# A hybrid decoder layer in float32: products moved from GpSimd to VectorE, two steps moved to a later place in the order

## The chip, the cores and the metric

The kernel runs on one core of one Trainium2 chip. The metric is the device time of one execution in microseconds, the median of several runs; lower is better. A profile of one execution, taken by the hardware, stands beside the times.

## What is computed

One decoder layer for 512 tokens of width 2048, float32. The normalised input goes through one wide projection; its columns feed two branches, whose outputs are gated, added, projected and added to the input. The reference, cut to what matters:

```python
xn = rmsnorm(h, norm_w); proj = xn @ w_in
# branch 1: gated linear recurrence, 8 heads of 128
f = lb + (1 - lb) * sigmoid(f_pre); k = 1 - f
#   S_t = diag(f_t) S_{t-1} + k_t i_t^T ;  o_t = S_t^T q_t
o_hg = rmsnorm(o, hg_norm_w) * silu(hg_z);  y_hg = o_hg @ w_branch_hg
# branch 2: sparse attention, 16 heads in 4 groups, rotation on 32 of 128 dims
p_cmp = masked_softmax(q @ kc.T);  o_cmp = p_cmp @ vc   # 31 compressed keys
p = masked_softmax(q @ ks.T);      o_slc = p @ vs       # selected blocks
p = masked_softmax(q @ kw.T);      o_win = p @ vw       # window
o_nsa = (g0 * o_cmp + g1 * o_slc + g2 * o_win) * silu(nsa_z)
y_nsa = o_nsa @ w_branch_nsa
h = h + (g_hg * y_hg + g_nsa * y_nsa) @ w_out;  return rmsnorm(h, final_norm_w)
```

With 512 tokens the selection takes every block that a query may see, so the selected and the window part are both causal attention, with different keys and values.

## The kernel before, in words

Every wide product keeps float32 accuracy by splitting each operand into a high part (a cast on ScalarE) and a low part (a subtraction on VectorE) and running three matmuls (`mm3`, L139 to L141). A chunk of weights, 128x1024 numbers, is loaded by SyncE's queue, cast on ScalarE (L130) and split on VectorE (L131); two chunks are held (`whl`). A chunk feeds eight units of three matmuls.

The stages, in order of time: the start (0 to 62 us) normalises four blocks of 128 tokens (`normalise`), transposes them and multiplies each with the first weight columns; then gates and values by a scheme with seven products for eight (to some 500 us); the recurrence, head by head; the compression of keys and values beside the recurrence's branch product; the attention, group by group (some 1130 to 1660 us); the branch product of the attention, the output product and the last normalisation.

Small work is woven into the projections: `weave` runs a generator of projection units and, after every few units, one step of a side generator. In the recurrence `hg_core(head)`, 17 steps, runs beside the 48 units of `hg_proj(head + 1)`. It builds decays over spans of 2, 4, ... 128 tokens: `grow` (L566 on GpSimd, L567 on VectorE) doubles a span, `decayed` (L576 on GpSimd, L577 on VectorE) makes the scaled operands `qk`, L601 multiplies them on TensorE, L605 puts the result into `ad` by a mask. Two levels share a bank of PSUM. Then come the states (L644 to L648), the output `po`, its square split in two, and, in the last step, the mean over the head by two matmuls with `ones` (L668, L669), the root on ScalarE (L670, with a load of its function table), the reciprocal (L671) and two products on VectorE (L672, L673), and the store.

In the attention `nsa_core(g)`, 48 steps, runs beside the projection of the next group, `nsa_proj(g + 1)`, or beside z and gate units. Per group: scores against the compressed keys and their softmax over `pc`; then per head four score steps (blocks i = 3, 2, 1, 0: scores into a bank of the two `sc` banks, mask and row maximum in one VectorE instruction L921, exponential on ScalarE L925, reciprocal and gate, scaling on GpSimd L930), and six steps that transpose the probabilities (L949), split them and multiply them with the values into `po`. `roped` rotates a projected head: a shuffle, the sine product on GpSimd (L698), cosine product and sum on VectorE. `raw` names rotating tiles of two buffers, used by rotations, z units and the compressed values (`vcz`), which are loaded from `vc_d` by ScalarE's queue.

A scheduler sets each engine's order ahead of time from the program; each engine then runs its instructions strictly in that order, and waits by semaphores.

Of the kernel before, what the change touches and what calls it, by code (L numbers as in the profile page):

```python
# [8 lines left out]
F32 = mybir.dt.float32  # L9
# [6 lines left out]
P = 128  # L16
S = 512
# [58 lines left out]
def body(tc, a, out):  # L76
# [216 lines left out]
    with pool("st_a") as sp:  # L293
# [29 lines left out]
        def normalise(i):  # L323
            x = xt[i]
            ss = sp.tile([P, 2], F32, name="ss", bufs=4)
            h0, h1 = slice(0, D // 2), slice(D // 2, D)
            sq = sp.tile([P, D // 2], F32, name="sq", bufs=1)
            sq2 = sp.tile([P, D // 2], F32, name="sq2", bufs=1)
            nc.scalar.activation(sq, x[:, h1], AF.Square, accum_out=ss[:, 1:2])
            nc.vector.scalar_tensor_tensor(sq2, x[:, h0], 1.0, x[:, h0], op0=OP.mult, op1=OP.mult,  # L330
                                           accum_out=ss[:, 0:1])
            for k0 in (8, 12):
                c = slice(k0 * P, (k0 + 4) * P)
                nc.gpsimd.tensor_tensor(x[:, c], x[:, c], nw[:, c], op=OP.mult)
            nc.vector.tensor_tensor(ss[:, :1], ss[:, :1], ss[:, 1:], op=OP.add)
            nc.scalar.activation(ss[:, :1], ss[:, :1], AF.Sqrt, scale=1.0 / D, bias=epst)
            nc.vector.reciprocal(ss[:, :1], ss[:, :1])
            for k0 in range(0, KD, 4):
                c = slice(k0 * P, (k0 + 4) * P)
                if k0 < 8:  # L340
                    nc.vector.scalar_tensor_tensor(x[:, c], x[:, c], ss[:, :1], nw[:, c], op0=OP.mult, op1=OP.mult)
                else:
                    nc.vector.tensor_scalar(x[:, c], x[:, c], ss[:, :1], None, op0=OP.mult)

# [158 lines left out]
    with pool("hg") as hp:  # L503
        hgw = sv[:, R_HGW:R_HGW + 1]
        heads = {}
        def values(pr):

# [32 lines left out]
        def hg_core(head):  # L540
# [18 lines left out]
            def grow(h):  # L559
# [5 lines left out]
                whole = lambda v: v[:, :, w - 1:w].to_broadcast([P, S // h, w])  # L565
                nc.gpsimd.tensor_tensor(fv[:, :, 0], fv[:, :, 0], whole(pv[:, :, 1]), op=OP.mult)  # L566
                nc.vector.tensor_tensor(pv[:, :, 1], pv[:, :, 1], whole(pv[:, :, 0]), op=OP.mult)  # L567

            def decayed(h):
# [5 lines left out]
                qk = hp.tile([P, S], F32, name="qk", bufs=3)  # L575
                nc.gpsimd.tensor_tensor(half(qk)[:, :, 0], half(kt)[:, :, 0], half(suf)[:, :, 0], op=OP.mult)  # L576
                nc.vector.tensor_tensor(up(tiles(qk)), up(q), up(tiles(pre)), op=OP.mult)  # L577
# [45 lines left out]
            qd = hp.tile([P, 3, P], F32, name="qd", bufs=2)  # L623
            nc.gpsimd.tensor_tensor(kd, kt[:, :3 * P], suf[:, :3 * P], op=OP.mult)
            nc.vector.tensor_tensor(qd, q[:, 1:], tiles(pre)[:, 1:], op=OP.mult)
# [11 lines left out]
            nc.scalar.copy(kn, ps[:, :3 * P])  # L637
            yield
            yield
            ps = lbank()  # L640
# [25 lines left out]
            yield  # L666
            pm = lbank()
            nc.tensor.matmul(pm, lhsT=ones, rhs=sh, start=True, stop=False)  # L668
            nc.tensor.matmul(pm, lhsT=ones, rhs=sl, start=False, stop=True)  # L669
            nc.scalar.activation(ob, pm, AF.Sqrt, bias=epst)  # L670
            nc.vector.reciprocal(ob, ob)  # L671
            nc.vector.scalar_tensor_tensor(ow, ow, hgw, ob, op0=OP.mult, op1=OP.mult)  # L672
            nc.vector.tensor_tensor(ow, ow, zs, op=OP.mult)  # L673
            nc.gpsimd.dma_start(ohg_d[head], ow)

# [17 lines left out]
    def roped(ap, acc, dst):  # L693
# [3 lines left out]
        nc.vector.stream_shuffle(sh, dst[:ROT], mask=list(range(16, 32)) + list(range(16)))  # L697
        nc.gpsimd.tensor_tensor(sh, sh, sin, op=OP.mult)  # L698
        nc.vector.tensor_tensor(dst[:ROT], dst[:ROT], cos, op=OP.mult)
# [119 lines left out]
    def nsa_proj(g):  # L819
        raw = ap.tile([P, 4, 2, DH], F32, name="vraw")  # L820
        for b in range(2):
            nc.scalar.dma_start(raw[:, :, b], v_d[1 + b, :, :, g * DH:(g + 1) * DH].rearrange("i p c -> p i c"))
        vh = ap.tile([P, 4, 2, DH], F32R, name="vh", bufs=2)
        vl = ap.tile([P, 4, 2, DH], F32R, name="vl", bufs=2)
        f = lambda t: t.rearrange("p j e c -> p (j e c)")
        split(f(vh), f(vl), f(raw))
        q = []
# [21 lines left out]
    def nsa_core(g):  # L849
# [47 lines left out]
        p3l = ap.tile([P, 2, HPG, P], F32R, name="p3l")  # L897
        o3 = ap.tile([P, HPG, P], F32, name="o3")
        for h in range(HPG):
            qh, ql = q[h]  # L900
            sc = {}
            for i in (3, 2, 1, 0):
# [29 lines left out]
            if h == 0:  # L932
                cmp_t()
                yield
            po = psum("po")
            mm3(po, vcz[0][:, h], vcz[1][:, h], ph, pl, True, False)
            pend = None

            def pv_mm(parts, hi, lo, last):
                for n, (j, b) in enumerate(parts):  # L940
                    w = slice(n * (4 - j) * P, (n + 1) * (4 - j) * P)
                    mm3(po[:, j * P:], vh[:, j, b], vl[:, j, b], hi[:, w], lo[:, w], False, last)

            for parts in (((3, 0), (3, 1)), ((2, 0), (2, 1)), ((1, 0),), ((0, 0),), ((1, 1),), ((0, 1),)):
                ps = tbank()
# [8 lines left out]
                else:  # L954
                    hi = ap.tile([P, o], F32R, name=f"pth{o}", bufs=o // 256)
                    lo = ap.tile([P, o], F32R, name=f"ptl{o}", bufs=o // 256)
                    split(hi, lo, ps[:, :o])
                    if pend:
                        pv_mm(*pend, False)
                    pend = (parts, hi, lo)  # L960
                yield
            pv_mm(*pend, True)
            ow = ap.tile([P, 384], F32, name="ow", bufs=2)
            nc.vector.tensor_copy(ow, po[:, :384])
            nc.scalar.copy(o3[:, h], po[:, 384:])
            nc.gpsimd.dma_start(ons_d[g * HPG + h][:, :384], ow)
            yield

        ps = sbank()
# [9 lines left out]
    for g in range(GROUPS - 1):  # L979
        weave(nsa_proj(g + 1), 128, nsa_core(g), 48)  # L980
    
# [3 lines left out]

    weave(last(), 112, nsa_core(GROUPS - 1), 48)
    nsa.close()
# [118 lines left out]
```

## Time and profile before

| | |
|---|---|
| median of 3 runs | 2109.39 us (2108.59 to 2112.3) |
| the profiled execution | 2108.82 us |
| its span, first to last instruction | 2106.7 us |
| TensorE busy | 2062.0 us, 98% |
| VectorE busy | 1209.0 us, 57%, 1875 instructions |
| ScalarE busy | 816.5 us, 39% |
| GpSimd busy | 322.4 us, 15%, 411 instructions |
| granted clock of TensorE | 0.996 of full |

A matmul is listed from its start to its modelled end, and the next one starts before that end; so the engine reads as busy until the last one in flight is through, and a wait shorter than that doesn't show. A float32 matmul that isn't split shows as two passes. The trace names for each idle time the instruction that ended it.

### The profile page before, as it was taken

The numbers are of one execution on the slowest core, as the hardware profiler recorded it, in microseconds if no ns is written. First come the engines' busy times: TensorE is split into PE (matmuls) and PEld (weight loads), VectorE is DVE, ScalarE is ACT, GpSimd is POOL, SyncE is SP. The second block draws the span as 40 slices with busy tenths as digits, with TensorE's granted clock in tenths as the row PEclk, the third lists the DMA queues.
The fourth block names the chain that finished last, engine by engine and source line by source line (L and its number), as shares of the span: only waits on it lengthen the run. The fifth ranks groups of instructions, "written<-read, shape, count | busy, mean of one in ns | idle before, by whom it ended". The sixth has DMA issues, their size and how long they took to land.

```text
span 2106.7 us, 26671 instructions
## 1 busy us (share of the span) xinstructions
PE 2062.0 (98%) x10304; PEld 1721.2 (82%) x10304; DVE 1209.0 (57%) x1875; ACT 816.5 (39%) x1267; POOL 322.4 (15%) x411
## 2 busy tenths in 40 slices
PE   7999999999999999999999999999999999999998
PEld 6888888888888778878888887877878888888887
DVE  7687778745456655566545665657654453433333
ACT  4454444532233233344323444445445432222232
POOL 2000000003233432100002222213212100000000
PEclk9999999999999999999999999999999999999999
DMA  6325243332323222566752222222223394445232
GB/s 184 100 105 180 100 152 114 121 101 74 96 83 93 76 76 85 167 188 202 247 164 85 74 73 85 68 84 64 78 75 92 90 304 132 149 140 212 98 130 90
DMA packets 306595, 254.46 MB, mean 121 GB/s; under 512 B 10666, under 2 KB 263411, under 8 KB 305827
## 3 DMA queue, kind: packets, MB, share of 16 engines
q1 hardware_dynamic: 282980, 202.55, 31.8%
q0 software_dynamic: 8096, 26.28, 3.4%
q10 hardware_dynamic: 15392, 23.92, 3.3%
q8 instruction: 81, 1.33, 0.3%
q14 instruction: 46, 0.38, 0.1%
HBM read 222.25 MB, written 30.47 MB: 120 GB/s over the span
## 4 chain that ended last, share of the span: by engine, by line
PE 82%; DVE 7%; issue 4%; ACT 3%; DMA 3%; POOL 1%; SPq 0%; ACTq 0%; DVEq 0%; POOLq 0%
PE pj L139 17%; PE pj L141 17%; PE pj L140 17%; PE sc L214 4%; PE pt L214 4%; PE sc L215 2%; PE pt L215 2%; PE sc L141 2%; PE sc L139 2%; PE sc L140 2%; PE po L140 1%; DVE whl L131 1%; PE po L139 1%; PE po L141 1%; PE pt L949 1%
## 5 line engine op out<-in xcount | busy, mean ns | idle before, releaser
L139 PE MATMUL pj<-xhl,whl 128*128 128x512 f32 x1344 | 538.5, 401 | 0.0
L141 PE MATMUL pj<-xhl,whl 128*128 128x512 f32 x1344 | 527.7, 393 | 0.8 <-DVE whl L131 0.8
L140 PE MATMUL pj<-xhl,whl 128*128 128x512 f32 x1344 | 525.2, 391 | 0.0
L131 DVE TENSOR_TENSOR whl<-wr,whl 128x1024 fp32r<-128x1024 f32 x244 | 303.8, 1245 | 373.2 <-ACT whl L130 372.5
L130 ACT CAST whl<-wr 128x1024 fp32r<-128x1024 f32 x244 | 256.5, 1052 | 563.3 <-PE pj L141 446.8
L141 PEld LDWEIGHTS pj<-xhl,whl 128*128 128x128 f32 x1344 | 252.3, 188 | 56.6 <-DVE whl L131 2.0
L140 PEld LDWEIGHTS pj<-xhl,whl 128*128 128x128 f32 x1344 | 252.9, 188 | 46.4
L139 PEld LDWEIGHTS pj<-xhl,whl 128*128 128x128 f32 x1344 | 252.7, 188 | 46.1
L135 ACT CAST whl<-xt 128x1024 fp32r<-128x1024 f32 x75 | 78.6, 1052 | 97.7 <-PE pt L215 33.1
L136 DVE TENSOR_TENSOR whl<-xt,whl 128x1024 fp32r<-128x1024 f32 x75 | 91.5, 1223 | 39.3 <-ACT whl L135 39.2
L930 POOL TENSOR_SCALAR s<-s,sm 128x512 f32<-128x512 f32 (+3 forms) x128 | 82.2, 655 | 149.4 <-DVE sm L928 89.9
L139 PE MATMUL pj<-onh,whl 128*128 128x512 f32 x256 | 99.6, 389 | 0.0
L140 PE MATMUL pj<-onl,whl 128*128 128x512 f32 x256 | 99.6, 389 | 0.0
L141 PE MATMUL pj<-onh,whl 128*128 128x512 f32 x256 | 99.6, 389 | 0.0
L136 DVE TENSOR_TENSOR ptl<-pt,pth 128x512 fp32r<-128x512 f32 (+1 forms) x80 | 50.5, 633 | 69.3 <-ACT pth L135 68.6
L925 ACT ACTIVATE s<-s,mx 128x512 f32<-128x512 f32 (+3 forms) x128 | 70.9, 555 | 43.8 <-DVE mx L923 39.0
L135 ACT CAST pth<-pt 128x512 fp32r<-128x512 f32 (+1 forms) x80 | 43.5, 544 | 96.1 <-PE pt L949 95.7
L201 DVE TENSOR_TENSOR xt<-xt 128x1024 f32<-128x1024 f32 x64 | 77.5, 1219 | 0.6
L921 DVE CUSTOM_DVE_ANT_0 s<-sc,cf 128x512 f32<-128x512 f32 (+3 forms) x128 | 59.3, 483 | 20.1 <-PE sc L141 19.4
L698 POOL TENSOR_TENSOR rsh<-rsh,rope 32x512 f32<-32x512 f32 x28 | 42.2, 1507 | 183.8 <-DVE rsh L697 166.3
L566 POOL TENSOR_TENSOR suf<-suf,pre 128x256 f32<-128x256 f32 x56 | 51.8, 926 | 116.7 <-DVE pre L549 94.6
L131 DVE TENSOR_TENSOR cl<-wr,ch 128x1024 fp32r<-128x1024 f32 x32 | 39.1, 1223 | 44.6 <-ACT ch L130 44.6
(431 smaller groups left out, 4004.9 us busy)
## 6 DMA issues: line engine op xcount, KB each, us to landing
wr<-in_w_in_dram SPq DMA_DIRECT2D x172, 512.0 KB
xt<-in_w_in_dram SPq DMA_DIRECT2D x32, 1024.0 KB
wr<-in_w_branch_nsa_dram SPq DMA_DIRECT2D x32, 512.0 KB
wr<-in_w_out_dram SPq DMA_DIRECT2D x32, 512.0 KB
wr<-in_cmp_k_w_dram SPq DMA_DIRECT2D x16, 512.0 KB
wr<-in_w_branch_hg_dram SPq DMA_DIRECT2D x16, 512.0 KB
wr<-in_cmp_v_w_dram SPq DMA_DIRECT2D x16, 512.0 KB
gat_d<-wr POOLq DMA_DIRECT2D x20, 256.0 KB, 3.0
```

The costliest lines, as they stand in the source:

```text
L130: nc.scalar.copy(hi[:, :n], raw[:, :n])
L131: nc.vector.tensor_tensor(lo[:, :n], raw[:, :n], hi[:, :n].bitcast(F32), op=OP.subtract)
L135: nc.scalar.copy(hi, src)
L136: nc.vector.tensor_tensor(lo, src, hi.bitcast(F32), op=OP.subtract)
L139: nc.tensor.matmul(acc, lhsT=lh, rhs=rh, start=start, stop=False, **kw)
L140: nc.tensor.matmul(acc, lhsT=lh, rhs=rl, start=False, stop=False, **kw)
L141: nc.tensor.matmul(acc, lhsT=ll, rhs=rh, start=False, stop=stop, **kw)
L201: nc.vector.tensor_tensor(dst, dst, more, op=OP.add)
L214: nc.tensor.matmul(av, lhsT=l0, rhs=r, start=start, stop=False, skip_group_check=True)
L215: nc.tensor.matmul(av[:, 0], lhsT=l1, rhs=r[:, 0], start=False, stop=stop, skip_group_check=True)
L925: nc.scalar.activation(s[:, b], s[:, b], AF.Exp, scale=SCALE, bias=mx[:, b:b + 1], accum_out=sm[:, b:b + 1])
L930: nc.gpsimd.tensor_scalar(s[:, b], s[:, b], sm[:, b:b + 1], 1.0, op0=OP.mult, op1=OP.mult)
```

## The change

- Start: all four products with the norm weight are on VectorE; before, two were on GpSimd and VectorE scaled their results.
- Recurrence: the GpSimd products of `grow`, `decayed` and `kd` are on VectorE. The normalisation of a head (two mean matmuls to the store) becomes a function that runs in the next head's step 13, between its `kd` transposes and its states; the last head's runs at its own end.
- Attention: sine product and scaling are on VectorE. The first bank of block i = 2 comes from the projection's three banks. The products of probabilities with values are put in a queue `due` and run one or two steps later; a head's last two run in the next head's score steps. The values of a group are loaded as two halves into `raw` tiles. A core has 46 steps.

```diff
-            for k0 in (8, 12):
-                nc.gpsimd.tensor_tensor(x[:, c], x[:, c], nw[:, c], op=OP.mult)
...
-                if k0 < 8:
-                    nc.vector.scalar_tensor_tensor(x[:, c], x[:, c], ss[:, :1], nw[:, c], op0=OP.mult, op1=OP.mult)
-                else:
-                    nc.vector.tensor_scalar(x[:, c], x[:, c], ss[:, :1], None, op0=OP.mult)
+                nc.vector.scalar_tensor_tensor(x[:, c], x[:, c], ss[:, :1], nw[:, c], op0=OP.mult, op1=OP.mult)
...
-                nc.gpsimd.tensor_tensor(fv[:, :, 0], fv[:, :, 0], whole(pv[:, :, 1]), op=OP.mult)
+                nc.vector.tensor_tensor(fv[:, :, 0], fv[:, :, 0], whole(pv[:, :, 1]), op=OP.mult)
...
-                nc.gpsimd.tensor_tensor(half(qk)[:, :, 0], half(kt)[:, :, 0], half(suf)[:, :, 0], op=OP.mult)
+                nc.vector.tensor_tensor(half(qk)[:, :, 0], half(kt)[:, :, 0], half(suf)[:, :, 0], op=OP.mult)
...
-            nc.gpsimd.tensor_tensor(kd, kt[:, :3 * P], suf[:, :3 * P], op=OP.mult)
+            nc.vector.tensor_tensor(kd, kt[:, :3 * P], suf[:, :3 * P], op=OP.mult)
...
             yield
+            if left:
+                left.pop()()
             yield
...
-            pm = lbank()
...
-            nc.gpsimd.dma_start(ohg_d[head], ow)
+            def normed():
+                pm = lbank()
...
+                nc.gpsimd.dma_start(ohg_d[head], ow)
+            left.append(normed)
+            if head == HG - 1:
+                left.pop()()
...
-        nc.gpsimd.tensor_tensor(sh, sh, sin, op=OP.mult)
+        nc.vector.tensor_tensor(sh, sh, sin, op=OP.mult)
...
-        raw = ap.tile([P, 4, 2, DH], F32, name="vraw")
-        for b in range(2):
-            nc.scalar.dma_start(raw[:, :, b], v_d[1 + b, :, :, g * DH:(g + 1) * DH].rearrange("i p c -> p i c"))
...
+        for b in range(2):
+            raw = ap.tile([P, S], F32, name="raw", bufs=2)
+            rv = raw.rearrange("p (i c) -> p i c", i=4)
+            nc.scalar.dma_start(rv, v_d[1 + b, :, :, g * DH:(g + 1) * DH].rearrange("i p c -> p i c"))
+            split(vh[:, :, b], vl[:, :, b], rv)
...
+        def pv_next():
+            if not due:
+                return
+            h, po, parts, hi, lo, last = due.pop(0)
+            for n, (j, b) in enumerate(parts):
+                w = slice(n * (4 - j) * P, (n + 1) * (4 - j) * P)
+                mm3(po[:, j * P:], vh[:, j, b], vl[:, j, b], hi[:, w], lo[:, w], False, last)
+            if last:
...
+                if i > 1:
+                    pv_next()
...
-                        ps = sbank()
+                        ps = bank() if i == 2 and b == 0 else sbank()
...
-                    nc.gpsimd.tensor_scalar(s[:, b], s[:, b], sm[:, b:b + 1], 1.0, op0=OP.mult, op1=OP.mult)
+                    nc.vector.tensor_scalar(s[:, b], s[:, b], sm[:, b:b + 1], None, op0=OP.mult)
...
+                    if m == 2:
+                        po = psum("po")
+                        mm3(po, vcz[0][:, h], vcz[1][:, h], ph, pl, True, False)
+                    elif m > 2:
+                        pv_next()
+                    due.append([h, None, parts, hi, lo, m == 5])
...
-        weave(nsa_proj(g + 1), 128, nsa_core(g), 48)
+        weave(nsa_proj(g + 1), 128, nsa_core(g), 46)
```

**The order of instructions.** Line numbers of the changed kernel are its own: `kt` to `qk` stand there at L542 to L572, the masked copies at L583 to L600, the normalisation at L667 to L672, the states at L641 to L645.

VectorE, the first operations of a head of the recurrence, before:

```order
L549 TENSOR_SCALAR pre<-sg,omlb,lbt 128x512
L552 TENSOR_TENSOR qf<-qf,pre 128x4x64
L671 RECIPROCAL ob<-ob 128x512
L567 TENSOR_TENSOR pre<-pre 128x256
L131 TENSOR_TENSOR whl<-wr,whl 128x1024
L672 SCALAR_TENSOR_TENSOR ow<-ow,sv,ob 128x512
L577 TENSOR_TENSOR qk<-qf,pre 128x128x2
L673 TENSOR_TENSOR ow<-ow,zs 128x512
L588 COPY_PREDICATED ad<-cm,sc 128x256
L567 TENSOR_TENSOR pre<-pre 128x128x2
L590 COPY_PREDICATED ad<-cm,sc 128x128
```

and now:

```order
L544 TENSOR_SCALAR pre<-sg,omlb,lbt 128x512
L547 TENSOR_TENSOR qf<-qf,pre 128x4x64
L561 TENSOR_TENSOR suf<-suf,pre 128x256
L562 TENSOR_TENSOR pre<-pre 128x256
L571 TENSOR_TENSOR qk<-kt,suf 128x128x2
L572 TENSOR_TENSOR qk<-qf,pre 128x128x2
L561 TENSOR_TENSOR suf<-suf,pre 128x128x2
L562 TENSOR_TENSOR pre<-pre 128x128x2
L571 TENSOR_TENSOR qk<-kt,suf 128x64x4
L572 TENSOR_TENSOR qk<-qf,pre 128x64x4
L131 TENSOR_TENSOR whl<-wr,whl 128x1024
L583 COPY_PREDICATED ad<-cm,pt 128x256
```

The reciprocal and the two products of the head before have left the place between the first links; the GpSimd products (`suf`, and `qk` from `kt`) stand in it.

VectorE, between the levels and the end of a head, before:

```order
L605 COPY_PREDICATED ad<-cm,pt 128x16x16
L131 TENSOR_TENSOR whl<-wr,whl 128x1024 x2
L537 TENSOR_TENSOR zs<-pj,zs 128x512
L648 SCALAR_TENSOR_TENSOR st<-st,pre,sc 128x128 x2
L131 TENSOR_TENSOR whl<-wr,whl 128x1024
L136 TENSOR_TENSOR sl<-ob,sh 128x512
```

and now:

```order
L619 TENSOR_TENSOR kd<-kt,suf 128x384
L600 COPY_PREDICATED ad<-cm,sc 128x16x16
L620 TENSOR_TENSOR qd<-qf,pre 128x384
L131 TENSOR_TENSOR whl<-wr,whl 128x1024 x2
L670 RECIPROCAL ob<-ob 128x512
L131 TENSOR_TENSOR whl<-wr,whl 128x1024
L671 SCALAR_TENSOR_TENSOR ow<-ow,sv,ob 128x512
L645 SCALAR_TENSOR_TENSOR st<-st,pre,sc 128x128
L672 TENSOR_TENSOR ow<-ow,zs 128x512
L645 SCALAR_TENSOR_TENSOR st<-st,pre,sc 128x128
L532 TENSOR_TENSOR zs<-pj,zs 128x512
L136 TENSOR_TENSOR sl<-ob,sh 128x512
```

The normalisation of the head before (L670 to L672) now stands ahead of and between the two state additions (L645).

VectorE at the start of the second group of the attention, before:

```order
L131 TENSOR_TENSOR whl<-wr,whl 128x1024
L179 TENSOR_TENSOR raw<-pj,raw 128x512
L876 TENSOR_TENSOR pc<-pt,cf 128x512
L136 TENSOR_TENSOR vczl<-raw,vczh 128x512
L877 TENSOR_REDUCE cst<-pc 128x16
L878 TENSOR_TENSOR pc<-pc,cst 128x512
L921 ISA s_9846,mx<-sc,cf 128x512
L921 ISA mx 128x1
L921 ISA s_9846,mx<-sc,cf 128x512
L921 ISA mx 128x1
```

and now, in two pieces with one weight split between them:

```order
L179 TENSOR_TENSOR raw<-pj,raw 128x512
L136 TENSOR_TENSOR vl<-raw,vh 128x4x128
L879 TENSOR_TENSOR pc<-pt,cf 128x512
L880 TENSOR_REDUCE cst<-pc 128x16
L881 TENSOR_TENSOR pc<-pc,cst 128x512
L942 ISA s_9847,mx<-sc,cf 128x512
L942 ISA mx 128x1
L136 TENSOR_TENSOR vl<-raw,vh 128x4x128
L942 ISA s_9847,mx<-sc,cf 128x512
L942 ISA mx 128x1
L944 TENSOR_SCALAR mx<-mx 128x2
L883 TENSOR_TENSOR pc<-pc,cf 128x512
```

```order
L884 TENSOR_REDUCE cst<-pc 128x16
L131 TENSOR_TENSOR whl<-wr,whl 128x1024
L136 TENSOR_TENSOR vczl<-raw,vczh 128x512
L885 TENSOR_SCALAR cst<-cst 128x16
L948 RECIPROCAL sm<-sm 128x2
L942 ISA s_9881,mx<-pj,cf 128x384
```

The split of the compressed values (`vczl`) has moved behind the row maxima of the first scores; the two splits of the group's values (`vl`) now wait for loads into `raw`. On ScalarE the cast of the second half of the values stands ahead of the exponential over `pc`, and the cast of the compressed values ahead of the first exponentials of the scores.

## Rows read from the trace of the kernel before

**Rows 1.** Stretches: length, busy PE, PEld, DVE, ACT, POOL (instructions), clock, DMA share, GB/s.
```profile
0.00:62.00 62.00, 49.81 (x284) 44.47 (x285) 49.25 (x66) 27.64 (x48) 14.60 (x14) 0.92 0.52 156
...
500.00:895.00 395.00, 387.25 (x2124) 323.20 (x2123) 226.91 (x312) 129.24 (x176) 114.82 (x124) 1.00 0.32 95
...
1130.00:1660.00 530.00, 518.10 (x2520) 428.28 (x2519) 316.96 (x775) 247.20 (x511) 128.72 (x182) 1.00 0.27 78
...
1850.00:1900.00 50.00, 50.00 (x222) 41.38 (x222) 18.61 (x22) 11.99 (x13) 0.00 (x0) 1.00 0.49 150
```

**Rows 2.** Waits of TensorE: who ended them, us in total, times, longest.
```profile
PE sc L139 <- DVE mx L921: 8.9, 6, 2.5
PE sc L601 <- DVE ad L605: 7.4, 7, 1.3
PE pt L349 <- DVE xt L341: 3.6, 1, 3.6
PE pt L349 <- issue: 3.4, 2, 1.8
PE pt L349 <- DVE xt L343: 1.7, 1, 1.7
PE sc L139 <- ACT fh L135: 1.7, 1, 1.7
PE po L140 <- DVE ptl L136: 1.6, 3, 0.5
PE po L139 <- ACT pch L135: 1.2, 2, 1.0
```

**Rows 3.** VectorE in order of time, a head of the recurrence: start, duration, instruction.
```profile
642.26 0.42 DVE L567 TENSOR_TENSOR pre<-pre 128x256 f32<-128x256 f32 x1 [0.56 <-POOL suf L566]
642.61 0.72 DVE L605 COPY_PREDICATED ad<-cm,sc 128x256 f32<-128x256 uint8 x1
```

**Rows 4.** TensorE in order of time, the level matmuls just behind that.
```profile
643.47 1.08 PE L601 MATMUL sc<-qk 128*128 128x64 f32 x8 [1.33 <-DVE ad L605]
```

**Rows 5.** ScalarE and VectorE in order of time, the start of an attention group.
```profile
1282.62 0.62 ACT L135 CAST vczh<-raw 128x512 fp32r<-128x512 f32 x1 [5.03 <-DMA raw<-vc_d]
...
1283.32 0.69 DVE L136 TENSOR_TENSOR vczl<-raw,vczh 128x512 fp32r<-128x512 f32 x1 [3.74 <-ACT vczh L135]
```

**Rows 6.** VectorE by line and shape: busy us, mean ns of one, idle before.
```profile
L131 DVE TENSOR_TENSOR whl<-wr,whl 128x1024 fp32r<-128x1024 f32 x244 | 303.8, 1245 | 373.2 <-ACT whl L130 372.5
...
L699 DVE TENSOR_TENSOR raw<-raw,rope 32x512 f32<-32x512 f32 x24 | 31.0, 1291 | 0.2
...
L671 DVE RECIPROCAL ob<-ob 128x512 f32<-128x512 f32 x8 | 26.8, 3346 | 0.7 <-ACT ob L670 0.7
...
L672 DVE SCALAR_TENSOR_TENSOR ow<-ow,sv,ob 128x512 f32<-128x512 f32 x8 | 9.5, 1192 | 0.0
...
L343 DVE TENSOR_SCALAR xt<-xt,ss 128x512 f32<-128x512 f32 x8 | 7.5, 974 | 1.9 <-POOL xt L334 1.9
...
L341 DVE SCALAR_TENSOR_TENSOR xt<-xt,ss,nw 128x512 f32<-128x512 f32 x8 | 5.9, 768 | 2.7 <-POOL nw L305 2.7
...
L547 DVE TENSOR_SCALAR kt<-sg,nomlb,omlb 128x512 f32<-128x512 f32 x8 | 4.3, 542 | 0.0
...
L335 DVE TENSOR_TENSOR ss<-ss 128x1 f32<-128x1 f32 x4 | 3.7, 925 | 1.7 <-ACT sq L329 1.5
...
L699 DVE TENSOR_TENSOR craw<-craw,rope 32x512 f32<-32x512 f32 x4 | 2.7, 678 | 1.1 <-DMA rope<-in_cf_dram 1.0
```

**Rows 7.** ScalarE in order of time, the end of a head of the recurrence.
```profile
671.29 1.05 ACT L130 CAST whl<-wr 128x1024 fp32r<-128x1024 f32 x1 [0.98 <-PE pj L141]
...
672.86 1.28 ACT L670 ACT_TABLE_LOAD   x1
674.15 0.69 ACT L670 ACTIVATE ob<-pt,epst 128x512 f32<-128x512 f32 x1
```

**Rows 8.** Issues of transfers in the attention: KB each, median us to landing.
```profile
z_d<-raw POOLq DMA_DIRECT2D x8, 256.0 KB, 3.2
```

More of the change, by code (lines that the diff above doesn't have):

```diff
@@ L331, in normalise @@
                                            accum_out=ss[:, 0:1])
-            for k0 in (8, 12):
-                c = slice(k0 * P, (k0 + 4) * P)
-                nc.gpsimd.tensor_tensor(x[:, c], x[:, c], nw[:, c], op=OP.mult)
             nc.vector.tensor_tensor(ss[:, :1], ss[:, :1], ss[:, 1:], op=OP.add)
@@ L505, in body @@
         heads = {}
+        left = []
         def values(pr):
@@ L666, in hg_core @@
             yield
-            pm = lbank()
[L668 to L673, printed above, removed]
-            nc.gpsimd.dma_start(ohg_d[head], ow)
+            def normed():
+                pm = lbank()
+                nc.tensor.matmul(pm, lhsT=ones, rhs=sh, start=True, stop=False)
+                nc.tensor.matmul(pm, lhsT=ones, rhs=sl, start=False, stop=True)
+                nc.scalar.activation(ob, pm, AF.Sqrt, bias=epst)
+                nc.vector.reciprocal(ob, ob)
+                nc.vector.scalar_tensor_tensor(ow, ow, hgw, ob, op0=OP.mult, op1=OP.mult)
+                nc.vector.tensor_tensor(ow, ow, zs, op=OP.mult)
+                nc.gpsimd.dma_start(ohg_d[head], ow)
+            left.append(normed)
+            if head == HG - 1:
+                left.pop()()
         weave(hg_proj(0), 0)
@@ L819, in nsa_proj @@
     def nsa_proj(g):
-        raw = ap.tile([P, 4, 2, DH], F32, name="vraw")
-        for b in range(2):
-            nc.scalar.dma_start(raw[:, :, b], v_d[1 + b, :, :, g * DH:(g + 1) * DH].rearrange("i p c -> p i c"))
         vh = ap.tile([P, 4, 2, DH], F32R, name="vh", bufs=2)
         vl = ap.tile([P, 4, 2, DH], F32R, name="vl", bufs=2)
-        f = lambda t: t.rearrange("p j e c -> p (j e c)")
-        split(f(vh), f(vl), f(raw))
+        for b in range(2):
[3 more added lines that the diff above has]
+            split(vh[:, :, b], vl[:, :, b], rv)
         q = []
@@ L898, in nsa_core @@
         o3 = ap.tile([P, HPG, P], F32, name="o3")
+        due = []
+        def pv_next():
[6 more added lines that the diff above has]
+            if last:
+                ow = ap.tile([P, 384], F32, name="ow", bufs=2)
+                nc.vector.tensor_copy(ow, po[:, :384])
+                nc.scalar.copy(o3[:, h], po[:, 384:])
+                nc.gpsimd.dma_start(ons_d[g * HPG + h][:, :384], ow)
         for h in range(HPG):
@@ L929, in nsa_core @@
                 for b in range(2):
-                    nc.gpsimd.tensor_scalar(s[:, b], s[:, b], sm[:, b:b + 1], 1.0, op0=OP.mult, op1=OP.mult)
+                    nc.vector.tensor_scalar(s[:, b], s[:, b], sm[:, b:b + 1], None, op0=OP.mult)
+                if h == 0 and i == 1:
+                    cmp_t()
                 yield
[L932 to L944, printed above, removed]
+            for m, parts in enumerate((((3, 0), (3, 1)), ((2, 0), (2, 1)), ((1, 0),), ((0, 0),), ((1, 1),), ((0, 1),))):
                 ps = tbank()
@@ L954, in nsa_core @@
                 else:
-                    hi = ap.tile([P, o], F32R, name=f"pth{o}", bufs=o // 256)
-                    lo = ap.tile([P, o], F32R, name=f"ptl{o}", bufs=o // 256)
+                    hi = ap.tile([P, o], F32R, name=f"pth{o}", bufs=2)
+                    lo = ap.tile([P, o], F32R, name=f"ptl{o}", bufs=2)
                     split(hi, lo, ps[:, :o])
-                    if pend:
-                        pv_mm(*pend, False)
-                    pend = (parts, hi, lo)
-                yield
[L962 to L966, printed above, removed]
+                    if m == 2:
[4 more added lines that the diff above has]
+                    due.append([h, None, parts, hi, lo, m == 5])
+                    if m >= 2:
+                        for d in due:
+                            d[1] = po
+                yield
+        while due:
             yield
+            pv_next()
+        yield
         ps = sbank()
@@ L984, in last @@
         yield from merge_gates(NG, NG + 6, ap, "raw")
-    weave(last(), 112, nsa_core(GROUPS - 1), 48)
+    weave(last(), 112, nsa_core(GROUPS - 1), 46)
     nsa.close()
```

## The prediction, made before the changed kernel was run

> **What bounds the kernel now.** I read the busy time by stage first. Late in the program, in the last branch product, nothing disturbs TensorE: 222 matmuls of 512 columns in 50 us, 0.225 us each, the clock at full speed [rows 1]. The same engine is busy for nearly all of every other stage, so the reader should look at what is missing: 12.2 us of 62 at the start, 7.8 of 395 in the recurrence, 11.9 of 530 in the attention [rows 1]. VectorE is busy for 57% of the recurrence and 60% of the attention. So the end is set by TensorE, and the only time to be had are its waits; work taken off GpSimd is worth nothing by itself.
>
> The second view is who TensorE waited for [rows 2]. Recurrence: 7.4 us, 7 times, L601 on VectorE's L605. Attention: 8.9 us in six waits of scores for a score bank (L139 on L921), 1.6 for low halves of probabilities, 1.2 for the compressed branch. Start: 3.6 until the norm weight is broadcast, then 3.4 and 1.7. Compression: 1.7, once. Third, I followed one wait of each kind. In the recurrence VectorE stood 0.56 us for GpSimd's `suf` product, then did `pre`, and only then emptied the bank of the level before [rows 3]; TensorE, 1.33 us idle, wanted that bank [rows 4]. So GpSimd is on the path there, through VectorE's queue. At the start of a group VectorE stood 3.74 us for the split of the compressed values, because ScalarE had stood 5.03 us for their load [rows 5].
>
> **The change part by part.** The profiled execution took 2108.8 us (span 2106.7 and 2.1 around it); the median of the runs is 0.6 above it.
>
> Start. VectorE now does four products with the weight per block of tokens, where it did two and two scalings after GpSimd. The eight scalings took 0.97 us each and four one-column sums 0.93 each while GpSimd ran [rows 6]; eight more products at about 0.77, as the two that stay, and sums that no longer wait at some 0.2 (an estimate: one column is next to nothing) make 7.8+3.7 into 6.2+0.8, 4.5 us less work on VectorE. Against it: in the first block the first low half of the weights now stands behind two more products, 1.5 us. The 3.6 us stay. Of the 5.1 us behind them at most all goes; at worst 2 us are added. I take 4, near the gain, since VectorE has hardly a pause in this stage (49 of 62 us, [rows 1]) and loses more work than it is held back.
>
> Recurrence, what goes. The three GpSimd products per level stand in VectorE's queue, so nothing there waits for GpSimd; in the order, the chain of the levels runs without the reciprocal between its first links. A level is then five operations of some 0.45 us, as the products and copies of [rows 3] are where nothing disturbs them (0.42), and a share of the weight split (1.25, [rows 6]), under 3 us, while TensorE has nine wide matmuls (2.0 us) and 0.9 us of its own per level. I count the 7.4 us as gone. Heads need some 6 us more of VectorE, 14 products at 0.45, in 44 us: 57% becomes about 70%, hidden.
>
> Recurrence, what comes. The normalisation of a head (reciprocal 3.35, product 1.19 [rows 6]) now runs between the state products of the next. VectorE's order there is reciprocal, weight split, product, first state addition; TensorE's third state product waits for that addition. Count from the end of the two mean matmuls. TensorE has 28 wide matmuls (6.3 us) and six small ones of two passes, 0.135 us a pass by [rows 4], 1.6: it comes to the wait after 7.9 us. The split waits for ScalarE's cast, which waits until the weight chunk in use is spent: 18 wide matmuls and two small, 4.6 us, the cast 1.05 as in [rows 7], then split 1.2, product 1.2, addition 0.35: 8.4 to 8.5 us. Through the root instead: table load 1.28 and root 0.69 [rows 7], reciprocal 3.35, split, product, addition: 8.1 plus latencies. So TensorE waits about 0.6; with the second addition behind one more product I take 0.7, times 8 heads 5.6. Bounds: 0 if the split comes early, 1.9 a head if VectorE comes to the reciprocal 2 us late. Net: -2, between -7.4 and +8.
>
> Rotation. The sine product moves to VectorE (28 x about 0.68), while its cosine product no longer runs beside GpSimd: 1.29 us then, 0.68 where it didn't [rows 6]. 19 us come, 15 go: nothing. In the compression stage the chain to the first frame gets shorter by the GpSimd hop: -0.5 of the 1.7.
>
> Attention. The scaling of probabilities costs VectorE 0.54 for 512 columns (a scaling of that shape, [rows 6]), by width 43 us for all 128, off GpSimd; with the rotation 60% becomes about 67%, hidden by TensorE's 530 us unless it bunches. The first score bank of the second block is now taken from the projection's three banks, and products of probabilities come one or two steps later, the last two in the next head. That removes the reason for 1.6 and most of 8.9. Not all: at a group's start the values are now loaded into the two rotating `raw` tiles, behind the store of the z unit, which takes 3.2 us to land [rows 8], and the compressed values wait for one of these tiles; in the new order VectorE and ScalarE each have a wait for such loads in their queue. The 3.74 us pause is then moved behind the first scores, but followed by the compressed probabilities that TensorE must transpose. Of the 11.7 us shown I let 8.5 go. Bounds: -11.7, and +3 if every group start is as late as the worst.
>
> Sum: -4 -2 -0.5 -8.5 = -15, from 2108.8 to 2093.8; as a median 2094.
>
> **Rivals.** (A) No new wait appears: all of 5.1, 7.4, 1.7 and 11.7 goes, 25.9 us: 2082.9, as a median 2083.5. For it: each is a queue that the change shortens. Against: the new queues above.
> (B) The reciprocal is the new wait, 1.9 us a head, 15 us in place of 7.4: +7.6, with the rest -5.4, 2104. It decides where VectorE comes more than about 1 us late to the reciprocal; two weight splits stand before it.
> (C) Slower: VectorE becomes the bound in the four score steps of a head. They hold the row maxima, scalings (2.7 us), a rotation chain (five operations of 0.7, 3.4) and one or two weight splits (1.25 each); with row maxima of about the scalings' size, 2.7 to 4, and small operations some 14 us, while TensorE needs some 12 (33 wide matmuls of the projection, 7.4, and about 4.5 of scores and values). If that excess of 2.3 us per head is not made up in the six transposing steps, where VectorE has less, but met at a bank, it costs 16 x 2.3 = 37 us in place of 11.7: +25, with the rest -6.5, 2127. It decides once VectorE is later than two steps, 5 us, behind.
> (D) Stores issued by GpSimd are held back by VectorE's new scalings, and the raw tiles come free late. A scaling pair is 1.1 us and a score step's set 2.7; at three group starts the latter is 8 us, nearly all that I took from the attention: 2102. The Trainium skill has the mechanism: SBUF — State Buffer, Who interferes with whom, says that tensor_scalar can enter a two-port mode that shuts GpSimd out of the shared ports, and with it the descriptors of its stores. No row here shows a store held back: issue to landing is 3.2 us in the median [rows 8]. By that page's 620 to 3100 ns my estimate would be 2.5 us a store, 7 us at three group starts.
>
> **How the numbers follow.** Chances: forecast 0.55, A 0.17, B 0.15, C 0.07, D 0.06. 0.2% is 4.2 us, about what a measurement here can tell: faster means below 2105. Forecast, A and D are faster, B half of the time: 0.84. Same is the middle of B, 0.07. Slower is C and B's end, 0.09. The range 2080 to 2107 holds the forecast, B, D and nearly all of A; it leaves out C and the ends of A and B.
>
> **What the new profile would show.** Right: no wait of the level matmuls (before: L601) for VectorE; no product of probabilities waiting for a low half; the 12.2 us idle of the start near 8. New waits of about 0.7 us at the third state product, and waits on transposes of compressed probabilities at group starts. Wrong: waits for weight splits in the attention (C), state products waiting for over 1.5 us (B), or group starts without any wait (A).

## The result, and the profile after

| | before | after |
|---|---|---|
| median | 2108.99 us (2107.38 to 2112.3) | 2085.39 us (2082.56 to 2087.05, 4 runs) |
| ratio to before, 95% interval | | 0.9885 [0.9867, 0.9903] |
| span of the profiled execution | 2106.7 us | 2085.2 us |
| VectorE busy | 1209.0 us | 1247.2 us |
| GpSimd busy | 322.4 us | 78.9 us |

The change makes the kernel 1.15% faster. The time lies inside the range of the prediction (2080 to 2107), 8.6 us below its likeliest value of 2094 and 1.9 above rival A's 2083.5. The profiled execution of the changed kernel is the longest of its four (2087.05 us), so the two spans differ by 21.5 us where the medians differ by 23.6.

Busy time by stretch in the changed kernel (columns as in [rows 1]; the stages come a few us earlier now):

```profile
0.00:62.00 62.00, 54.35 (x310) 48.92 (x311) 46.71 (x74) 27.41 (x49) 3.34 (x6) 0.92 0.52 156
500.00:895.00 395.00, 391.07 (x2135) 328.37 (x2134) 249.80 (x429) 132.89 (x183) 11.76 (x22) 1.00 0.35 99
1130.00:1660.00 530.00, 525.45 (x2579) 438.35 (x2578) 345.17 (x928) 250.19 (x522) 20.86 (x37) 1.00 0.29 82
1850.00:1900.00 50.00, 50.00 (x222) 41.39 (x222) 18.85 (x22) 11.98 (x13) 0.00 (x0) 1.00 0.45 139
```

TensorE misses 7.7 us of the start instead of 12.2, 3.9 of the second stretch instead of 7.8, 4.6 of the third instead of 11.9. Of the 3.9 us, 3.7 are the wait for the compression's first frame, which now falls into this stretch. VectorE rises to 63% and 65% of the second and third: more work, and hidden. Who TensorE waited for, in the changed kernel (compare [rows 2]):

```profile
PE sc L139 <- ACT fh L135: 3.7, 1, 3.7
PE pt L343 <- DVE xt L337: 3.1, 1, 3.1
PE pj L139 <- ACT wfh L130: 2.4, 1, 2.4
PE pt L895 <- DVE pc L888: 1.7, 2, 1.0
PE sc L139 <- DVE mx L942: 1.4, 1, 1.4
PE pj L141 <- DVE whl L131: 1.3, 3, 0.5
PE sc L215 <- DVE eh L136: 1.3, 2, 0.8
PE pt L895 <- DVE sm L948: 1.3, 1, 1.3
```

The 7.4 us of the level matmuls are gone (L601 before, L596 now: no line). The 8.9 us for score banks are 1.4. Transposes of the compressed probabilities (L895) are new, 3.0 us. One wait has grown: the first compression matmul waits 3.7 us for the cast of the frame (`fh`), where it waited 1.7. At the start the transposes behind the first wait hardly any more, and a wait of 2.4 us for the cast of the first weights (`wfh`) is new.

To place gains in stages I cut each trace at the same events of TensorE. S: start to the first matmul of the recurrence. R: seven head periods. L: first matmul of the last head to the first compression matmul. C: from there to the first score matmul of the first group (against the compressed keys). A: to the attention's branch product. The rest is 358.0 us in every run. The kernel before was timed again beside each batch of kernels and read 2109.5 to 2112.2 us there, so the ratio compares better than the median.

| kernel | S | R | L | C | A | median | ratio to before |
|---|---|---|---|---|---|---|---|
| before | 481.5 | 328.8 | 89.1 | 240.5 | 608.9 | 2108.99 | |
| after | 477.6 | 320.1 | 92.0 | 239.9 | 597.5 | 2085.39 | 0.9885 [0.9867, 0.9903] |
| products_only | 475.5 | 320.8 | 90.8 | 239.7 | 606.1 | 2092.44 | 0.9911 [0.9896, 0.9926] |
| order_only | 481.9 | 320.8 | 89.7 | 242.6 | 599.3 | 2092.36 | 0.9909 [0.9895, 0.9924] |
| u_rec_pool | 476.3 | 320.7 | 91.7 | 240.4 | 596.7 | 2084.69 | 0.9873 [0.9859, 0.9888] |
| u_norm_end | 475.0 | 320.8 | 90.4 | 239.4 | 597.9 | 2082.9 | 0.9867 [0.9851, 0.9883] |
| u_start_pool | 479.6 | 320.1 | 92.1 | 241.0 | 597.0 | 2088.99 | 0.9901 [0.9886, 0.9916] |
| u_scale_pool | 475.1 | 320.1 | 92.2 | 239.8 | 600.4 | 2086.86 | 0.9892 [0.9878, 0.9907] |
| u_bank | 473.3 | 320.1 | 91.5 | 239.5 | 598.5 | 2084.5 | 0.9884 [0.9867, 0.99] |
| u_pv | 474.0 | 320.1 | 91.8 | 240.2 | 598.6 | 2084.12 | 0.9883 [0.9868, 0.9898] |
| fill10 | 477.3 | 320.2 | 90.7 | 236.4 | 597.9 | 2081.84 | 0.9869 [0.9856, 0.9883] |
| own_tile | 476.7 | 320.2 | 91.4 | 238.3 | 605.2 | 2091.54 | 0.9917 [0.9903, 0.993] |
| both | 478.6 | 320.2 | 90.9 | 237.4 | 604.2 | 2086.81 | 0.9896 [0.9882, 0.9909] |
| early_load | 475.2 | 320.1 | 90.9 | 235.5 | 592.6 | 2075.06 | 0.9831 [0.9818, 0.9845] |

Reading scale: A of the five kernels with the attention code of the changed one (after, u_rec_pool, u_norm_end, u_start_pool, fill10) lies between 596.7 and 597.9. S scatters far more (below), so parts are judged by their own stage, not by the median. The 21.5 us between the two spans are S -3.8, R -8.7, L +3.0, C -0.5, A -11.4. The cuts shift some work: in the new order the two mean matmuls of the seventh head run behind R, in the eighth head (0.5 us from R to L), and in the changed kernel eight projection matmuls that stood in C stand in L (1.8 us).

### The profile page after: what moved, and what is told of

Its sections match the earlier page's. It is cut to its first block, busy times and chain, and to the rows that moved or that the text cites. A ratio compares the mean times of both kernels' runs of the same rounds, so it can differ in the third digit from the quotient of the medians.

```text
span 2085.2 us, 26314 instructions
## 1 busy us (share of the span) xinstructions
PE 2057.3 (99%) x10304; PEld 1723.8 (83%) x10304; DVE 1247.2 (60%) x2147; ACT 813.8 (39%) x1271; POOL 78.9 (4%) x135
## 4 chain that ended last, share of the span: by engine, by line
PE 37%; issue 16%; DMA 2%; DVE 1%; ACT 1%; POOL 1%; ACTq 0%; SPq 0%; DVEq 0%; POOLq 0%
PE pj L141 9%; PE pj L140 9%; PE pj L139 9%; PE sc L139 2%; PE sc L140 2%; PE sc L141 2%; PE po L139 1%; PE po L141 1%; PE po L140 1%; DMA zr<-z_d 1%; PE pt L139 1%; PE pt L140 1%; PE pt L141 1%; PE pt L960 1%; DMA wr<-in_cmp_v_w_dram 0%
## 5 line engine op out<-in xcount | busy, mean ns | idle before, releaser
L131 DVE TENSOR_TENSOR whl<-wr,whl 128x1024 fp32r<-128x1024 f32 x244 | 298.2, 1222 | 394.1 <-ACT whl L130 393.9
L136 DVE TENSOR_TENSOR whl<-xt,whl 128x1024 fp32r<-128x1024 f32 x75 | 91.5, 1223 | 39.9 <-ACT whl L135 39.8
L131 DVE TENSOR_TENSOR cl<-wr,ch 128x1024 fp32r<-128x1024 f32 x32 | 39.2, 1225 | 49.6 <-ACT ch L130 49.4
L942 DVE CUSTOM_DVE_ANT_0 s<-sc,cf 128x512 f32<-128x512 f32 (+3 forms) x112 | 51.1, 475 | 27.9 <-PE sc L141 27.9
L130 ACT CAST ch<-wr 128x1024 fp32r<-128x1024 f32 x32 | 33.6, 1049 | 61.5 <-PE sc L141 43.3
L139 PEld LDWEIGHTS pj<-onh,whl 128*128 128x128 f32 x256 | 48.0, 188 | 10.1
L141 PEld LDWEIGHTS pj<-onh,whl 128*128 128x128 f32 x256 | 48.0, 188 | 10.0
```

What stands on the lines that cost most here:

```text
L130: nc.scalar.copy(hi[:, :n], raw[:, :n])
L131: nc.vector.tensor_tensor(lo[:, :n], raw[:, :n], hi[:, :n].bitcast(F32), op=OP.subtract)
L136: nc.vector.tensor_tensor(lo, src, hi.bitcast(F32), op=OP.subtract)
L139: nc.tensor.matmul(acc, lhsT=lh, rhs=rh, start=start, stop=False, **kw)
L141: nc.tensor.matmul(acc, lhsT=ll, rhs=rh, start=False, stop=stop, **kw)
L942: nc.vector.tensor_tensor_reduce(out=s[:, b], in0=pb[b], in1=mk, scale=1.0, scalar=NEG, op0=OP.add, op1=OP.max, accum_out=mx[:, b:b + 1])
```

## The experiments

**The two halves.** One kernel has only the products on VectorE, in the old order; the other has the new order, with all products left on GpSimd.

products_only, on the kernel before:
```diff
# shortened: the operations alone, not the lines
-  nc.gpsimd.tensor_tensor(...) / nc.gpsimd.tensor_scalar(s[:, b], ...)   # start, recurrence, rotation, scaling
+  nc.vector.tensor_tensor(...) / nc.vector.tensor_scalar(s[:, b], ...)
```


> The kernel before with the products alone moved to VectorE (start, recurrence, sine, scaling); normalisation, products of probabilities, score banks and value tiles as before. Theory Q (GpSimd's products hold TensorE up through VectorE's queue): the start gains 3 to 4 us, the 7.4 us of waits of the level matmuls go to under 2, the attention gains 1 to 3 because its waits for score banks stay: 2094 to 2100. Rival O (where the long normalisation and the products of probabilities stand in the order is what counts, whichever engine does the products): the start's 3 to 4 us alone, the level matmuls still wait over 5 us behind the reciprocal: 2103 to 2107.

order_only, on the kernel after: the same lines from `nc.vector` back to `nc.gpsimd`.

> The changed kernel with all moved products back on GpSimd (start, recurrence, sine, scaling); only the order, the third score bank and the value tiles are changed. Theory Q: no gain at the start, the level matmuls keep 4 us or more of their 7.4 us of waits, the attention gains 5 to 9: 2096 to 2102. Rival O: recurrence and attention gain nearly all that they gained in the change, 8.7 and 11.4 us: 2088 to 2092.

Measured: each half gives 0.9% alone, together 1.15%. In R each half has the whole gain (320.8 both; 320.1 together), so neither theory holds there: each part alone is enough. The attention is divided: the products bring 2.9 us, the order 9.7. TensorE's waits in the attention of products_only, then of order_only:

```profile
PE sc L139 <- DVE mx L915: 9.1, 5, 2.5
```
```profile
PE pt L901 <- DVE mx L950: 2.9, 4, 1.2
PE sc L139 <- DVE mx L948: 2.1, 1, 2.1
```

The waits for score banks need the new order; moving products leaves them as they were.

**Undoing one part in the recurrence.** u_rec_pool puts `grow`, `decayed` and `kd` back on GpSimd; u_norm_end lets each head normalise at its own end.

```diff
-                nc.vector.tensor_tensor(fv[:, :, 0], fv[:, :, 0], whole(pv[:, :, 1]), op=OP.mult)
+                nc.gpsimd.tensor_tensor(fv[:, :, 0], fv[:, :, 0], whole(pv[:, :, 1]), op=OP.mult)
... # the same for the product into qk and for kd
```


> The changed kernel with the recurrence's products alone back on GpSimd. Theory Q: VectorE waits for GpSimd before it empties the level's bank, TensorE waits again 4 to 8 us: 2090 to 2093. Rival O: the chain has room without the reciprocal, no wait comes back: 2085 to 2087.

```diff
-            if left:
-                left.pop()()
...
-            left.append(normed)
-            if head == HG - 1:
-                left.pop()()
+            normed()
```


> The changed kernel with the normalisation of a head back at the end of its own head, the products staying on VectorE. Theory Q: the 5 us of the normalisation stand in the chain of the levels, but that chain has about 5 us to spare: 0 to 2 us slower than the changed kernel, 2085 to 2088. Rival O: the level matmuls wait again, 6 to 9 us: 2091 to 2095.

Measured: R 320.7 and 320.8 against 320.1, and no level matmul waits in either. Two things stood in VectorE's queue ahead of the bank that TensorE wanted, the wait for GpSimd [rows 3] and the reciprocal of 3.35 us between the first links; taking away either is enough. The wait that I had expected at the third state product exists in no kernel with the new order, so the move of the normalisation costs nothing there; with the products on VectorE it brings at most 0.7 us of R, of which 0.5 are the two mean matmuls that fall behind R.

**Undoing one part at the start and in the attention.**

u_start_pool, the start's products back to the old form:
```diff
+            for k0 in (8, 12):
+                nc.gpsimd.tensor_tensor(x[:, c], x[:, c], nw[:, c], op=OP.mult)
... # and VectorE scales these two, as before
```


> The changed kernel with the start's second half of products with the norm weight back on GpSimd. If the start's gain comes from these products: the first projection ends some 3 us later, 2088 to 2090. If it comes from elsewhere (another order of loads): 2084 to 2087.

u_scale_pool, the scaling of probabilities back on GpSimd:
```diff
-                    nc.vector.tensor_scalar(s[:, b], s[:, b], sm[:, b:b + 1], None, op0=OP.mult)
+                    nc.gpsimd.tensor_scalar(s[:, b], s[:, b], sm[:, b:b + 1], 1.0, op0=OP.mult, op1=OP.mult)
```


> The changed kernel with the scaling of probabilities back on GpSimd. Theory Q: transposes come steps after the scaling, so nothing waits for GpSimd; VectorE gets 43 us of 530 back but its two-input operations wait beside GpSimd: within 2 us of the changed kernel, 2084 to 2088. Rival (the scaling's latency on GpSimd held up transposes): 3 to 8 us slower, 2088 to 2094.

u_bank, both score banks of block i = 2 from the two:
```diff
-                        ps = bank() if i == 2 and b == 0 else sbank()
+                        ps = sbank()
```


> The changed kernel with both score banks of the second block from the two sc banks, as before. If the third bank removes the waits for score banks: 4 to 8 us come back as waits of score matmuls for row maxima, 2089 to 2094. If the later place of the products of probabilities removes them: 2085 to 2087.

u_pv, products of probabilities at their old place, 48 steps a core:
```diff
-                if i > 1:
-                    pv_next()
...
+                    if pend:
+                        pv_mm(*pend, False)
+                    pend = (parts, hi, lo)
... # the transposes of the compressed probabilities go back to a step of their own, too
```


> The changed kernel with the products of probabilities at their old place, one step behind their transposes and all within their head; third bank and scaling on VectorE stay. If the delay is what removes TensorE's waits for low halves: 2 to 5 us slower, 2087 to 2091, with waits of po matmuls for ptl. If it removes the waits for score banks too: 6 us slower or more.

Measured: with the old start the first projection ends at 60.8 us in u_start_pool, 60.4 in order_only and 61.4 in the kernel before; with the new one at 56.6 to 58.8 in all eleven kernels. The start is worth some 3 to 4 us. Scaling on GpSimd costs 2.8 us of A. The transposes of the compressed probabilities then wait 3.5 us, for other instructions than the 3.0 us above, and scores wait 2.5 us for banks in place of 1.4; 1.0 of the 2.8 us is busy time and shows in no wait:

```profile
PE pt L895 <- DVE mx L944: 3.5, 4, 1.9
```

The third bank and the delayed products are worth 1.0 and 1.1 us, hardly outside the scatter of A. Without the third bank some waits for score banks come back (u_bank), but the 3.0 us of the transposes go:

```profile
PE sc L139 <- DVE mx L942: 3.9, 3, 2.6
```

Without the delay no product of probabilities waits for a low half (`ptl`), so the sign that I had named for it is missing. As in the recurrence, each edit could hide the other; own_tile, below, has both and is only 0.9 us of A faster than products_only, which has neither. So these two edits, which I thought would bring the attention's gain, are not what brought most of it.

**What is left, and the value tiles.** fill10 runs ten units of the branch product between the first frame and the first compression matmul. own_tile gives the values tiles of their own again, out of `raw` (for space `vraw` and `ow` have one buffer). The kernel called both has the two edits.

```diff
+        filled(10)
```


> The changed kernel with ten units of the value projection put ahead of the first compression matmuls. There TensorE now waits 3.7 us for the first frame, whose cast stands on ScalarE behind a weight cast that waits 5.3 us for its load. If the wait is the frame's lateness: it goes, 2 to 4 us faster, 2081 to 2084. If it is the stage's loads (two weight streams through three tiles): the wait moves to a weight cast and the time stays, 2084 to 2087.

```diff
-            raw = ap.tile([P, S], F32, name="raw", bufs=2)
+            raw = ap.tile([P, S], F32, name="vraw", bufs=1)
...
-                ow = ap.tile([P, 384], F32, name="ow", bufs=2)
+                ow = ap.tile([P, 384], F32, name="ow", bufs=1)
```


> The changed kernel with a tile of its own for the values of a group, in place of the rotating raw tiles (one buffer of the store tile ow is given up for the room). If the loads into raw tiles cause the remaining waits at group starts (the transposes of the compressed probabilities, 3.0 us): they go, 2 to 3 us faster, 2082 to 2084. If the compressed values' own load causes them: 2084 to 2087.

> Both of these. If each removes its wait: 5 to 7 us faster than the changed kernel, 2078 to 2081; if neither: 2084 to 2087.

Measured for fill10: no wait for `fh`; C falls by 3.5 us and L by 1.3, as the first expectation said. The grown wait comes from the order on ScalarE. In the changed kernel the frame's casts stand behind a weight cast that waits for its load (ScalarE in order of time):

```profile
888.34 1.04 ACT L130 CAST whl<-wr 128x1024 fp32r<-128x1024 f32 x1 [5.26 <-DMA wr<-in_w_in_dram]
889.29 1.30 ACT L135 CAST fh<-fr 128x248 fp32r<-128x248 f32 x4
```

In the kernel before, a cast of the frame stood ahead and waited for VectorE itself:

```profile
898.88 1.37 ACT L135 CAST fh<-fr 128x248 fp32r<-128x248 f32 x3 [2.37 <-DVE fr L753]
900.92 1.05 ACT L130 CAST whl<-wr 128x1024 fp32r<-128x1024 f32 x1 [0.67 <-DMA wr<-in_w_in_dram]
```

Measured for own_tile: 7.7 us of the attention are given back, 3.3 at the second group and 4.5 at the third. That is the opposite of what I had read into the shared tiles, and neither expectation held (2091.54). The kernel with both edits comes to 2086.81: the gain of fill10 in C (237.4) and the loss of own_tile in A (604.2) stand side by side. VectorE at the second group, first of own_tile, then of the changed kernel:

```profile
1264.13 0.69 DVE L880 TENSOR_REDUCE cst<-pc 128x16 f32<-128x512 f32 x1
1269.16 0.69 DVE L136 TENSOR_TENSOR vczl<-raw,vczh 128x512 fp32r<-128x512 f32 x1 [4.34 <-ACT vczh L135]
1269.77 0.68 DVE L881 TENSOR_TENSOR pc<-pc,cst 128x512 f32<-128x512 f32 x1
1270.37 0.68 DVE L942 CUSTOM_DVE_ANT_0 s<-sc,cf 128x512 f32<-128x512 f32 x1
```
```profile
1264.09 0.69 DVE L136 TENSOR_TENSOR vl<-raw,vh 128x512 fp32r<-128x512 f32 x1 [0.80 <-ACT vh L135]
...
1269.06 0.69 DVE L942 CUSTOM_DVE_ANT_0 s<-sc,cf 128x512 f32<-128x512 f32 x1 [0.55 <-PE sc L141]
...
1274.77 0.69 DVE L136 TENSOR_TENSOR vczl<-raw,vczh 128x512 fp32r<-128x512 f32 x1
```

The values in `raw` hold the rotating tile for longer, so the compressed values are loaded later (the loads are issued from 1268.3 us on, in own_tile from 1258.8) and the scheduler puts their split behind the first row maxima. With own tiles the split stands ahead of them again and VectorE stands still. In the fourth group no later group's values are loaded, and there the changed kernel has the old picture:

```profile
1534.64 0.69 DVE L136 TENSOR_TENSOR vczl<-raw,vczh 128x512 fp32r<-128x512 f32 x1 [6.29 <-ACT vczh L135]
1535.25 0.68 DVE L879 TENSOR_TENSOR pc<-pt,cf 128x512 f32<-128x512 f32 x1
```

**Taking the cause away.** The last kernel is fill10 with the compressed values loaded one stage early, in `nsa_proj`, into a tile of their own.

```diff
+        raw = ap.tile([P, S], F32, name="craw", bufs=1)
+        nc.gpsimd.memset(raw, 0.0)
+        for h in range(HPG):
+            nc.scalar.dma_start(raw[h * 32:h * 32 + NC, h * DH:(h + 1) * DH], vc_d[...])
+        groups[g] = vh, vl, q, kh, kl, raw
...
-                ow = ap.tile([P, 384], F32, name="ow", bufs=2)
+                ow = ap.tile([P, 384], F32, name="ow", bufs=1)
```


> Edit: the kernel with ten fillers ahead of the compression, and the compressed values of a group loaded one stage early, into a tile of their own, while the group before is still computed (the space comes from giving the output tile ow one buffer). Theory 1, the wait for the load of the compressed values in VectorE's queue is what the start of a group loses: in the changed kernel TensorE is idle 1.0, 0.6 and 2.7 us in the first 23 us of the second, third and fourth group; with the load done early VectorE's wait for the cast of the compressed values (6.3 us in the fourth group) goes, the attention falls from 597.9 with the fillers to 594 to 596 us, and the time to 2078 to 2080. Theory 2, the single buffer of ow is what cost the kernel with own value tiles its 7.7 us, and not the place of that wait: attention near 604, time near 2088. Theory 3, the queue is filled by other work and the wait hides: attention 597 to 598, time 2082.

Measured: 2075.06 us, faster than the changed kernel and fill10 (the intervals of the ratios don't meet). A falls to 592.6, 5.3 below fill10, more than the 4.3 that the idle time at the group starts had shown. early_load has the one-buffer `ow` too, so that isn't what cost own_tile its time; whether the one buffer of `vraw` has a share in it was not tested. The split no longer waits in the attention, and TensorE's longest wait there is short (waits of early_load, columns as above):

```profile
PE pj L141 <- DVE whl L131: 1.7, 3, 0.8
```

VectorE's waits for the cast of the compressed values, one row of each kernel's waits: before, products_only, own_tile, order_only, after. early_load has one of 1.2 us, at 1070 us, ahead of the attention.

```profile
DVE vczl L136 <- ACT vczh L135: 16.5, 3, 6.9
```
```profile
DVE vczl L136 <- ACT vczh L135: 17.3, 3, 7.2
```
```profile
DVE vczl L136 <- ACT vczh L135: 14.2, 3, 6.3
```
```profile
DVE vczl L136 <- ACT vczh L135: 7.0, 1, 7.0
```
```profile
DVE vczl L136 <- ACT vczh L135: 6.3, 1, 6.3
```

The attentions of these five take 608.9, 606.1, 605.2, 599.3 and 597.5 us, early_load's 592.6: three such waits go with 605 us and more, one with 597 to 599, none in the attention with 593.

## Why the prediction was right in sign and range, and where its sum failed

| term | forecast | measured |
|---|---|---|
| start (S) | -4 | -3.8 |
| recurrence (R) | -2 | -8.7 |
| compression (L and C) | -0.5 | +2.4 |
| attention (A) | -8.5 | -11.4 |
| sum | -15 | -21.5 |

The forecast's recurrence has eight heads, R seven; the eighth, and its 1.1 us of the 7.4, lies in L.

**Bound.** That TensorE's waits are all there is to gain, and that VectorE's extra work stays hidden, held: 38 us more of VectorE, and no wait for a split of the projections' weights (L131) above 0.5 us. Rival C is refuted by that.

**Start.** Right in sign and size, and by the start's own edit: u_start_pool gives it back. That -3.8 meets -4 so closely is luck: S scatters by 5.3 us between kernels with the same start, and 2.9 us of new waits (2.4 for `wfh`, which the forecast doesn't have, and 0.5 for the low half, where it counted 1.5) are nearly made up by 2.5 us of other waits that went and that it hadn't counted.

**Recurrence.** The step that failed is "So TensorE waits about 0.6 ... I take 0.7, times 8 heads 5.6". That wait is zero: with it left out, the sum would have been 2088. VectorE in the changed kernel, a head's end:

```profile
652.90 3.35 DVE L670 RECIPROCAL ob<-ob 128x512 f32<-128x512 f32 x1 [1.25 <-ACT ob L669]
657.29 1.23 DVE L131 TENSOR_TENSOR whl<-wr,whl 128x1024 fp32r<-128x1024 f32 x1 [1.04 <-ACT whl L130]
658.43 0.75 DVE L671 SCALAR_TENSOR_TENSOR ow<-ow,sv,ob 128x512 f32<-128x512 f32 x1
659.09 0.34 DVE L645 SCALAR_TENSOR_TENSOR st<-st,pre,sc 128x128 f32<-128x128 f32 x1
```

TensorE at the same place, the second mean matmul and the third state product:

```profile
651.74 0.39 PE L668 MATMUL pt<-sl,ones 128*128 128x512 f32 x1
...
659.85 0.38 PE L641 MATMUL sc<-vt,kn 128*128 128x128 f32 x2
```

From the end of the mean matmuls (652.13) VectorE has the first addition done after 7.3 us, where I counted 8.4 to 8.5; TensorE comes after 7.7, where I counted 7.9. The split comes 5.2 us after that end, not 5.65, and the product takes 0.75 us, not 1.2: its price in [rows 6] was that beside GpSimd's products, which the same change takes away. I had allowed for that in the rotation, and not here. The new place alone would have done it: in order_only, with the products still on GpSimd, this product takes 0.745 us. Rival B, the same wait at 1.9 us, falls with it.

The gain is even larger than the shown waits, and beyond my bound of -7.4. The seven periods of R, before and after:

```profile
481.45:810.27 328.82, 322.48 (x1824) 270.21 (x1823) 189.87 (x267) 103.74 (x145) 102.17 (x115) 1.00 0.28 82
```
```profile
477.62:797.72 320.10, 320.10 (x1823) 270.71 (x1822) 199.04 (x367) 101.95 (x143) 9.59 (x18) 1.00 0.30 84
```

Idle time falls by 6.3 us and busy time by 2.4: 0.5 for the two mean matmuls that fall behind R, 1.9 with the same matmuls. My reading is that part of each wait had been covered by the modelled end of the matmul in flight; no run shows it by itself.

**Compression.** The term was 2.9 us off. I followed the chain to the frame through VectorE and didn't ask what would stand ahead of its cast on ScalarE: the wait is 3.7 us, not the 1.2 that I left of it. fill10, without that wait, has 4.8 us less in L and C than the changed kernel.

**Attention.** The size was off by 2.9 us and half of the reason was wrong. All of A, before and after:

```profile
1139.79:1748.73 608.94, 596.62 (x2868) 492.75 (x2866) 352.98 (x805) 273.09 (x542) 131.59 (x189) 1.00 0.33 98
```
```profile
1129.67:1727.21 597.54, 591.89 (x2868) 492.33 (x2866) 378.82 (x956) 273.80 (x548) 24.10 (x43) 1.00 0.35 102
```

Idle falls by 6.7 us (I said 8.5), busy by 4.7 with 2868 matmuls in both. That the split of the compressed values moves behind the first scores and leaves waits on compressed probabilities came as forecast. But I put the gain down to the third bank and the delayed products, which bring some 1 us each, and counted the shared `raw` tiles as what keeps group starts late; they are what moves the split, and own_tile, without them, loses 7.7 us.

**Rivals A and D.** A comes nearest. Its condition, no new wait anywhere, holds at the state products, but not everywhere: the compression came to +2.4 where A has -1.7, and 4.4 us of waits are left in the attention (score banks and compressed probabilities). That its sum is close is in part luck, since the recurrence gained more than A counts. For D the store of the z unit lands sooner than before (2.7 us, [rows 8] 3.2), with all scalings on VectorE:

```profile
z_d<-raw POOLq DMA_DIRECT2D x8, 256.0 KB, 2.7
```

The longest of the eight took 5.6 us, before the change 6.0. The hold-up of GpSimd's stores that the Trainium skill (SBUF — State Buffer, Who interferes with whom) describes does not show in these stores.

**Open.** L and C together grow by 2.4 us: 2.0 more of the wait for `fh`, 0.5 for the two mean matmuls, less the 1.1 of the eighth head's level wait. The other 1 us is busy time that no wait explains; fill10 doesn't have it. Nor was a kernel tried that loads early without the fillers, or one without the third bank and the delayed products together.

## What to carry to other kernels

A load whose consumer stands early in an engine's queue can hold up all the work behind that consumer, not only its own result (5.3 us of the attention here): look for the instruction that waits at the head of the queue, and move its load a stage earlier. When a change takes one engine's work from beside another's, price the operations that stay at their undisturbed duration, in every term. Two parts of a change can remove the same wait; only a run with each alone tells it.

## What was not expected of the hardware

- TensorE's shown waits can understate what there is to gain. With the waits its busy time fell too, for the same matmuls: by 1.9 us of 322 in the recurrence and 4.7 of 597 in the attention. It isn't so everywhere: in S idle time fell by some 4.5 us and busy time rose by 0.7.
- VectorE's operations beside GpSimd's arithmetic took 1.55 to 1.9 times as long. Mean of one, after (the values before are 1192 ns of L672 and 1291 of L699 in [rows 6]; `qk` from `qf`, 128x256, had 653):

```profile
L671 DVE SCALAR_TENSOR_TENSOR ow<-ow,sv,ob 128x512 f32<-128x512 f32 x8 | 6.0, 744 | 0.0
...
L702 DVE TENSOR_TENSOR raw<-raw,rope 32x512 f32<-32x512 f32 x24 | 16.1, 672 | 0.0
...
L572 DVE TENSOR_TENSOR qk<-qf,pre 128x256 f32<-128x256 f32 x48 | 20.2, 420 | 0.0
```

- The time up to the recurrence scatters by 5.3 us (S from 473.3 to 478.6) between kernels whose code is the same up to there, more than most of the single edits are worth.
